# Shifting the weight tiles by 16 and 48 bytes, and the streamed tiles to multiples of 64 bytes

## The chip, the cores and the metric

The kernel runs on one core of one Trainium2 chip. The metric is the device time in microseconds (us) of one execution, the median of several runs; smaller is better. The profiled execution shown here is one further execution of the same program, with a time stamp for each instruction.

## What is computed

One decoder block for a sequence of 512 tokens with width 1024, in float32, depth 1. Cut to what matters:

```python
h = rms_norm(x, g_mix)
u, q, k, v, gate = split(h @ w_in)                 # 1024 x 3072
y = concat(causal_pool(u), diff_attention(rope(q), rope(k), v))
x = x + (y * sigmoid(gate)) @ w_out
x = x + cross_attention(rms_norm(x, g_cross), rms_norm(mem, g_mem), w_cq, w_ckv) @ w_co
x = x + square(relu(rms_norm(x, g_mlp) @ w_up)) @ w_down   # 1024 x 4096 x 1024
out = rms_norm(x, g_final)
```

## The kernel before, in words

Almost all of the time goes into matrix products. To keep float32 precision on TensorE, each operand is split into two parts, `hi` (the value rounded to the matmul's float32r type) and `lo` (the rest), and each product is made of three matmuls: hi x hi, hi x lo, lo x hi. That is `mm3`, lines 94, 95 and 96. A matmul consists of two instructions: a weight load (LDWEIGHTS) puts a 128 x 128 stationary block into the array, and the MATMUL then streams the moving operand, here 512 columns per partition (256 in some stages). The weight load for the next matmul runs while the present one streams.

Weights come in blocks of 128 x 1024 (512 KB). `load` (line 134) brings a block into a `wraw` buffer by a DMA of SyncE's queue; `prep` (line 144) splits it: ScalarE writes `whi` (line 100), VectorE writes `wlo` (line 101). There are three buffers each of `wraw`, `whi` and `wlo`. `weights` keeps the loads three blocks ahead and the splits two blocks ahead of use. `tile_mm` (line 240) runs one block: eight k-slices of 128 columns, three matmuls each, 24 matmuls in all, weights stationary, activations moving.

The stages in order: the V projection (`v_proj`, 4 blocks: here the activations `xg` are stationary and the weight parts are moving, 96 matmuls); 20 blocks of the table `PLAN` (q, k, gate and pooling projections, moving `xg`, 480 matmuls) with the attention work threaded in between; the output projection (moving `mix`, 192); memory keys (stationary weights, moving `s`, 256 columns wide, 192); memory values (`mem_v`, stationary `s`, moving weight parts, 96); cross attention's query projection (moving `xg`, 192), its scores (`mix` moving, `s` stationary, 256 wide, 96) and its products with the values (`at` moving, `mix` stationary, 48); its output projection (moving `xg`, 192); and the MLP in four groups, each of eight up blocks (moving the normed operand, which lies in `mix`, 192 matmuls) and eight down blocks (moving the activations, which lie in `xg`, 192; the last block of all is done in two halves of 256 columns).

The instruction order on TensorE is written by hand (the code's order); the other engines follow through semaphores.

**Where the tiles lie.** All SBUF tiles come from one pool. They are laid one behind the other in the order in which a tag is first asked for, each buffer rounded up to a multiple of 32 bytes per partition. A tile of 4 bytes (`eps`, `[P, 1]`) therefore takes 32 bytes and moves all that follows by half of 64, until the next such tile (`gsub`, `[P, 1]`) moves it back. In the program before, the start addresses modulo 64 are:

| tile | role in matmuls | start mod 64 |
|---|---|---|
| `tmp`, `cst` | moving in small products, transposes | 0 |
| `onef`, `ones`, `ss`, `wraw` | `ones` stationary in the norm sums | 32 |
| `xg` | moving (q, k, gates, pooling, cq, co, down); stationary in `v_proj` | 32 |
| `whi`, `wlo` | stationary; moving in `v_proj` and `mem_v` | 32 |
| `rstd`, `vr` | `vr` stationary in attention | 32 |
| `s`, `at`, `mix` | moving and stationary; `mix` moving in out and up | 0 |

Slices of a tile begin at multiples of 512 bytes, so they keep the tile's value. "Base" below means this start address modulo 64.

Of the kernel before, what the change touches and what calls it, by code (L numbers as in the profile page):

```python
# [12 lines left out]
F32R = mybir.dt.float32r  # L13
# [4 lines left out]
P = 128  # L18
T = 512
D = 1024  # L20
# [7 lines left out]
EPS = 1e-6  # L28
# [18 lines left out]
def block_kernel(ctx: ExitStack, tc: tile.TileContext, x0g, xT, memT, wv, wm, wckv, wpool, vecs, csts, outT):  # L47
# [14 lines left out]
    def nm(s):  # L62
        uid[0] += 1
        return f"{s}_{uid[0]}"

    def sb(tag, shape, bufs, dt=F32):
        return pool.tile(shape, dt, tag=tag, name=nm(tag), bufs=bufs)

    def tmp(dt=F32):
        return sb("tmp", [P, T], 10, dt)  # L70
# [13 lines left out]
    def f(ap):  # L84
        return ap.bitcast(F32)

    V = nc.vector
# [11 lines left out]
    def split(hi, lo, src, eng=V):  # L99
        S.copy(hi, src)  # L100
        eng.tensor_tensor(lo, src, f(hi), op=ALU.subtract)  # L101
# [11 lines left out]
    warm = ps("acc", 2)  # L113
    for j in range(WARM):
        nc.tensor.matmul(warm, idle[:, :P], idle, start=j == 0, stop=j == WARM - 1)
    eps = sb("eps", [P, 1], 1)
    V.memset(eps, EPS)
    one_f = sb("onef", [P, P], 1)
    V.memset(one_f, 1.0)
    ones = sb("ones", [P, P], 1, F32R)  # L120
    V.tensor_copy(ones, one_f)

# [1 line left out]
    blocks = []  # L124

    def add(src):
# [5 lines left out]
    def load(i):  # L132
        if i >= len(blocks) or i in raw:
            return
        r = sb("wraw", [P, D], 3)
        if i == 0:
            nc.sync.dma_start(r[:, :T], blocks[i][:, :T])
            load_x(1)
            nc.sync.dma_start(r[:, T:], blocks[i][:, T:])
        else:  # L140
            nc.sync.dma_start(r, blocks[i])
        raw[i] = r

    def prep(i):
        if i >= len(blocks) or i in ready:
            return
        load(i)
        hi = sb("whi", [P, D], 3, F32R)
        lo = sb("wlo", [P, D], 3, F32R)
        if i == 0:  # L150
            V.tensor_copy(hi[:, :T], raw[i][:, :T])
            V.tensor_tensor(lo[:, :T], raw[i][:, :T], f(hi[:, :T]), op=ALU.subtract)
            split(hi[:, T:], lo[:, T:], raw[i][:, T:])
        else:
            split(hi, lo, raw[i], G if i in WPOOL else V)
        ready[i] = (hi, lo)
# [5 lines left out]
            prep(j)  # L162
        return ready.pop(i)

# [1 line left out]
    def rsqrt(dst, ssum, scale, v, l, by=None):  # L166
        """dst = (ssum * scale + EPS) ** -0.5, times by(y) for a first factor; v and l are scratch"""
        V.tensor_scalar(v, ssum, scale, EPS, op0=ALU.mult, op1=ALU.add)
        S.activation(l, ssum, AF.Ln, bias=eps, scale=scale)
        S.activation(dst, l, AF.Exp, scale=-0.5)  # L170
        S.activation(l, dst, AF.Square)
        V.scalar_tensor_tensor(l, l, -0.5, v, op0=ALU.mult, op1=ALU.mult)
        if by is not None:
            by(dst)
        V.scalar_tensor_tensor(dst, l, 1.5, dst, op0=ALU.add, op1=ALU.mult)
# [38 lines left out]
        S.activation(hi, src, AF.Copy, scale=g)  # L214
        V.scalar_tensor_tensor(lo, src, g, f(hi), op0=ALU.mult, op1=ALU.subtract)

# [1 line left out]
    clock = [0]  # L218
    due = []

# [24 lines left out]
                first and n == 0, last and n == len(ks) - 1)  # L245
            tick()

# [1 line left out]
    WU, WQ, WK, WGATE, WOUT, WCQ, WCO = 0, 4, 8, 12, 20, 28, 36  # L249
    WUP = 44  # L250
    WDN = WUP + 32
# [25 lines left out]
    def W(*key):  # L277
        return weights(where[key])

# [1 line left out]
    xr = {0: vx[:, NG_COL:]}  # L281
    xg = {}
    ss = sb("ss", [P, T], 1)
# [18 lines left out]
            load(k // 2)  # L302
    nc.sync.dma_start(cst, csts)

# [1 line left out]
    def lambdas():  # L306
        lvec = tmp()[:, :NVEC]
        nc.gpsimd.dma_start(lvec, vecs)
        lam = sb("lam", [P, 4], 1)
        lsum = sb("lsum", [P, 4], 1)  # L310
        for j in range(2):
            b = 128 * j
            V.tensor_tensor(lvec[:, b:b + 64], lvec[:, b:b + 64], lvec[:, b + 64:b + 128], op=ALU.mult)
            V.tensor_reduce(lsum[:, j:j + 1], lvec[:, b:b + 64], axis=AX.X, op=ALU.add)
            S.activation(lam[:, j:j + 1], lsum[:, j:j + 1], AF.Exp)
        V.tensor_tensor(lam[:, 2:3], lam[:, 0:1], lam[:, 1:2], op=ALU.subtract)
        V.tensor_scalar(lam[:, 3:4], lam[:, 2:3], LAM_INIT, None, op0=ALU.add)
        gsub = sb("gsub", [P, 1], 1)
        V.tensor_scalar(gsub, vec[:, GSUB:GSUB + 1], 1.0 - LAM_INIT, None, op0=ALU.mult)
        st["lam"], st["gsub"] = lam[:, 3:4], gsub  # L320

# [1 line left out]
    def v_proj():  # L323
        o = [ps("sc", 3), ps("sc", 3), ps("sc", 3), ps("av", 1)]
        tbs = [slice(i * P, (i + 1) * P) for i in range(NT)]
        for b in range(4):
            wh, wl = W("v", b)
            for kk in range(2):
                k = 2 * b + kk
                if k not in xg:  # L330
                    x_in(k)
                c = slice(kk * T, (kk + 1) * T)
                for i, tb in enumerate(tbs):
                    nc.tensor.matmul(o[i], xg[k][0][:, tb], wh[:, c], start=k == 0, stop=False)  # L334
                for i, tb in enumerate(tbs):
                    nc.tensor.matmul(o[i], xg[k][1][:, tb], wh[:, c], start=False, stop=False)  # L336
                for i, tb in enumerate(tbs):
                    nc.tensor.matmul(o[i], xg[k][0][:, tb], wl[:, c], start=False, stop=k == KC - 1)  # L338
                accumulate(ss, k, xr[k])
        sp = split_sq(ss, T)  # L340

        def stats():
            r = rstd_full(sp, ss)
            st["rstd"] = r
            rr = rstd_rows(sp, NT)
            V.tensor_tensor(cos_r, cos_r, r, op=ALU.mult)
            V.tensor_tensor(sin_r, sin_r, r, op=ALU.mult)
            vs = []
            for i in range(NT):
                vh = sb("vr", [P, T], 8, F32R)  # L350
                vl = sb("vr", [P, T], 8, F32R)
                scaled(vh, vl, o[i], rr[:, 2 * i:2 * i + 1])
                vs.append((vh, vl))
            st["v"] = vs
            lambdas()

        after(3, stats)

# [1 line left out]
    def qk_proj(which, h):  # L360
        o = acc()
        tile_mm(o, W(which, h), xg)
# [16 lines left out]
            nc.sync.dma_start(f(z[bot, :, :]), f(s[top, :, :]))  # L379
            st["z", h] = z  # L380

# [1 line left out]
    def scores(h, i):  # L383
        q, k, z = st["q", h], st["k", h], st["z", h]
        n = P * (i + 1)
# [50 lines left out]

        after(FINISH, finish)

# [1 line left out]
    gate, mixed, pooled = {}, {}, {}  # L440

    def gate_proj(m):
# [18 lines left out]
        split(pr[:, 0, :], pr[:, 1, :], y, MLO_E if m < 4 else V)  # L461
        mixed[m] = (pr[:, 0, :], pr[:, 1, :])

# [1 line left out]
    def pool_weights():  # L465
        r = sb("wraw", [P, D], 3)[:, :T]
        nc.sync.dma_start(r, wpool)
# [44 lines left out]
                after(START + SPACE * j, scores, j // NT, j % NT)  # L512
        tiles[kind](m)

# [1 line left out]
    res = {}  # L516

    def residual(m, o, g=None, ss=None, nxt=None, tag=None):
# [23 lines left out]
            tile_mm(o, W(key, m), rhs, early + late)  # L542
            done(m, o)

# [1 line left out]
    def mem_in():  # L546
        mg = {}
        sm = sb("ssm", [P, M], 1)
# [44 lines left out]
            scaled(p[:, 0, :], p[:, 1, :], o[i], st["mrow"][:, 2 * i:2 * i + 1])  # L593
            st["mv", half, i] = (p[:, 0, :], p[:, 1, :])

# [1 line left out]
    ss1 = sb("ss", [P, T], 1)  # L597
    x1g = {}

# [15 lines left out]

    after(STAT1, stats1)

# [1 line left out]
    cross_o = {}  # L619

    def cross_scores(h):
# [81 lines left out]

    after(STAT2, stats2)

# [1 line left out]
    ss3 = sb("ss", [P, T], 1)  # L707
    y3 = {}

    def last_rows(m, o, c):  # L710
        """Columns c of the last residual tile, then the final norm of those tokens."""
        w = c.stop - c.start
        V.tensor_tensor(res[m][:, c], o[:, c], res[m][:, c], op=ALU.add)
        sq = tmp()[:, :w]
        S.activation(sq, res[m][:, c], AF.Square)
        S.activation(y3[m // 2][:, 1, c], res[m][:, c], AF.Copy, scale=vec[:, G_FINAL + m:G_FINAL + m + 1])  # L716

        def norm():
            s = ps("tr", 2)[:, :w]
            nc.tensor.matmul(s, ones, st["sp3"][0][:, c], start=True, stop=False)  # L720
            nc.tensor.matmul(s, ones, st["sp3"][1][:, c], start=False, stop=False)
            nc.tensor.matmul(s, one_f, sq, start=False, stop=True)
            r, v, l = tmp()[:, :w], tmp()[:, :w], tmp()[:, :w]
            with tc.high_priority():
                S.activation(l, s, AF.Ln, bias=eps, scale=1.0 / D)
                S.activation(r, l, AF.Exp, scale=-0.5)
                V.tensor_scalar(v, s, 1.0 / D, EPS, op0=ALU.mult, op1=ALU.add)
                V.tensor_tensor(l, r, r, op=ALU.mult)
                V.scalar_tensor_tensor(l, l, -0.5, v, op0=ALU.mult, op1=ALU.mult)
                V.scalar_tensor_tensor(r, l, 1.5, r, op0=ALU.add, op1=ALU.mult)  # L730
            for j in range(KC // 2):
                for i in range(2):
                    eng = G if 2 * j + i in ON_POOL[c.start > 0] else V
                    eng.tensor_tensor(y3[j][:, i, c], y3[j][:, i, c], r, op=ALU.mult)  # L734
                nc.sync.dma_start(outT[:, 2 * j:2 * j + 2, c], y3[j][:, :, c])

        after(4, norm)

    for g in range(NG):
# [10 lines left out]
        for m in range(KC):  # L750
            last = g == NG - 1
# [3 lines left out]
            if last and m == KC - 1:  # L755
                st["sp3"] = split_sq(ss3, T)
                for hf, o in enumerate((ps("sc", 3), ps("sc", 3))):
                    c = slice(hf * M, (hf + 1) * M)
# [7 lines left out]
            if last:  # L766
                accumulate(ss3, m, res[m])
                S.activation(y3[m // 2][:, m % 2, :], res[m], AF.Copy,
                             scale=vec[:, G_FINAL + m:G_FINAL + m + 1])
# [70 lines left out]
```

## Time and profile before

| | us |
|---|---|
| median of 3 runs | 746.96 |
| lowest, highest | 746.91, 747.18 |
| span of the profiled execution (first to last instruction) | 744.6 |

The profiled execution's own time beyond its span is not given; the median is 2.4 us above the span, which is what lies around the instructions.

How to read the profile: PE is TensorE's matmul, PEld its weight load, DVE VectorE, ACT ScalarE, POOL GpSimd, SP SyncE. `L94 PE MATMUL acc<-mix,whi 128*128 128x512 f32 x296 | 117.0, 395` is a group: line 94, output tile `acc`, inputs `mix` (moving) and `whi` (stationary), 296 instructions, 117.0 us busy, 395 ns the mean of one. Matmuls are pipelined, and a matmul's shown duration reaches into the next one's; what one matmul costs is the distance from its start to the next start. That distance is read from the timeline view, whose first two columns are the start and the duration in us.

### The profile page before, as it was taken

What the parts mean: (1) busy time and instruction counts of PE and PEld (TensorE: products, weight loads), DVE (VectorE), ACT (ScalarE), POOL (GpSimd) and SP (SyncE); (2) the same over time, 40 slices, a digit from 0 to 9 for tenths busy, and PEclk for the clock granted to TensorE, in tenths of its full rate; (3) what the DMA queues carried; (4) which work ended last, traced back from release to release, by engine and by line L of the source; (5) the groups of instructions that cost most, each with busy time, mean ns of one, the idle gap of its engine ahead of it and who ended that gap; (6) DMA issues with size and microseconds to landing.
All of it is one profiled execution on the core that took longest, in us unless ns stands there. A gap on an engine that the chain in (4) does not pass through costs nothing.

```text
span 744.6 us, 8888 instructions
## 1 busy us (share of the span) xinstructions
PE 726.1 (98%) x3384; PEld 598.4 (80%) x3384; DVE 430.2 (58%) x677; ACT 354.9 (48%) x589; POOL 58.7 (8%) x50
## 2 busy tenths in 40 slices
PE   8999999999999999999999999999999999999993
PEld 6878888788889888888888888888888888888882
DVE  7587899875978556564664433443334533345436
ACT  7498997776765435344453411333214422234332
POOL 0053113533000000000000000000000000000003
PEclk9999999999999999999999999999999999999997
DMA  8343223241535531201323223233232232222203
GB/s 320 132 124 103 85 72 113 86 165 62 189 99 188 181 136 58 85 29 42 129 85 111 87 89 110 85 92 106 85 112 86 85 112 86 97 101 86 85 0 113
DMA packets 24650, 78.41 MB, mean 105 GB/s; under 512 B 2688, under 2 KB 4736, under 8 KB 24608
## 3 DMA queue, kind: packets, MB, share of 16 engines
q1 hardware_dynamic: 24560, 77.73, 32.0%
q8 instruction: 26, 0.43, 0.3%
q14 instruction: 16, 0.13, 0.1%
q0 software_dynamic: 48, 0.13, 0.0%
HBM read 73.65 MB, written 2.10 MB: 102 GB/s over the span
## 4 chain that ended last, share of the span: by engine, by line
PE 88%; ACT 5%; DVE 4%; DMA 1%; issue 1%; POOL 0%; SPq 0%; DVEq 0%; ACTq 0%
PE acc L94 25%; PE acc L96 24%; PE acc L95 24%; PE sc L96 3%; PE sc L94 3%; PE sc L95 3%; ACT tmp L395 1%; DVE mix L734 1%; DMA tmp<-xT 1%; ACT whi L100 1%; PE sc L334 1%; PE sc L336 1%; PE sc L338 1%; ACT tmp L365 1%; DVE tmp L393 1%
## 5 line engine op out<-in xcount | busy, mean ns | idle before, releaser
L100 ACT CAST whi<-wraw 128x1024 fp32r<-128x1024 f32 (+1 forms) x128 | 133.9, 1047 | 301.6 <-PE acc L95 233.2
L94 PE MATMUL acc<-xg,whi 128*128 128x512 f32 x504 | 198.6, 394 | 0.0
L96 PE MATMUL acc<-xg,wlo 128*128 128x512 f32 x504 | 196.7, 390 | 0.0
L95 PE MATMUL acc<-xg,whi 128*128 128x512 f32 x504 | 196.2, 389 | 0.0
L101 DVE TENSOR_TENSOR wlo<-wraw,whi 128x1024 fp32r<-128x1024 f32 (+1 forms) x128 | 158.2, 1236 | 32.3 <-ACT whi L100 31.2
L94 PE MATMUL acc<-mix,whi 128*128 128x512 f32 x296 | 117.0, 395 | 0.0
L96 PE MATMUL acc<-mix,wlo 128*128 128x512 f32 x296 | 116.9, 395 | 0.0
L95 PE MATMUL acc<-mix,whi 128*128 128x512 f32 x296 | 116.9, 395 | 0.0
L96 PEld LDWEIGHTS acc<-xg,wlo 128*128 128x128 f32 x504 | 94.6, 188 | 20.2
L94 PEld LDWEIGHTS acc<-xg,whi 128*128 128x128 f32 x504 | 94.7, 188 | 19.0
L95 PEld LDWEIGHTS acc<-xg,whi 128*128 128x128 f32 x504 | 94.7, 188 | 18.7
L520 DVE TENSOR_TENSOR vr<-acc,vr 128x512 f32<-128x512 f32 x41 | 28.3, 691 | 109.6 <-PE acc L96 109.6
L745 DVE SCALAR_TENSOR_TENSOR tmp<-acc,rstd 128x512 f32<-128x512 f32 x32 | 22.2, 693 | 87.6 <-PE acc L96 87.5
L96 PEld LDWEIGHTS acc<-mix,wlo 128*128 128x128 f32 x296 | 55.5, 187 | 13.6
L94 PEld LDWEIGHTS acc<-mix,whi 128*128 128x128 f32 x296 | 55.5, 187 | 13.5
L95 PEld LDWEIGHTS acc<-mix,whi 128*128 128x128 f32 x296 | 55.5, 187 | 13.5
L734 POOL TENSOR_TENSOR mix<-mix,tmp 128x256 f32<-128x256 f32 x7 | 6.1, 903 | 552.1 <-ACT mix L716 550.9
L101 DVE TENSOR_TENSOR xg<-tmp,xg 128x512 fp32r<-128x512 f32 x32 | 22.1, 692 | 0.3 <-ACT xg L100 0.3
L395 ACT ACTIVATE tmp<-tmp,small 128x128 f32<-128x128 f32 (+3 forms) x32 | 17.9, 560 | 5.8 <-DVE small L393 5.6
L100 ACT CAST xg<-tmp 128x512 fp32r<-128x512 f32 x32 | 19.8, 621 | 0.9
L746 ACT ACTIVATE tmp<-tmp 128x512 f32<-128x512 f32 x32 | 20.2, 633 | 0.0
L211 DVE TENSOR_TENSOR ss<-ss,tmp 128x512 f32<-128x512 f32 x27 | 18.5, 686 | 1.6 <-ACT tmp L210 1.4
(229 smaller groups left out, 945.1 us busy)
## 6 DMA issues: line engine op xcount, KB each, us to landing
wraw<-wm SPq DMA_DIRECT2D x108, 512.0 KB, 3.3
wraw<-wckv SPq DMA_DIRECT2D x16, 512.0 KB, 3.9
s<-s SPq DMA_DIRECT2D x8, 256.0 KB, 3.6
vr<-xT SPq DMA_DIRECT2D x8, 256.0 KB, 4.8
outT<-mix SPq DMA_DIRECT2D x8, 256.0 KB, 2.2
tmp<-xT SPq DMA_DIRECT2D x7, 256.0 KB, 6.7
wraw<-wv SPq DMA_DIRECT2D x3, 512.0 KB, 7.0
tmp<-memT SPq DMA_DIRECT2D x4, 256.0 KB, 4.7
```

Of the source, the lines that this page charges most:

```text
L94: nc.tensor.matmul(o, lh, rh, start=start, stop=False)
L95: nc.tensor.matmul(o, lh, rl, start=False, stop=False)
L96: nc.tensor.matmul(o, ll, rh, start=False, stop=stop)
L100: S.copy(hi, src)
L101: eng.tensor_tensor(lo, src, f(hi), op=ALU.subtract)
L211: V.tensor_tensor(ss, ss, sq, op=ALU.add)
L334: nc.tensor.matmul(o[i], xg[k][0][:, tb], wh[:, c], start=k == 0, stop=False)
L395: S.activation(e[:, :n], e[:, :n], AF.Exp, bias=mn, scale=-1.0, accum_out=sm[:, c:c + 1])
L520: V.tensor_tensor(t, o, t, op=ALU.add)
L734: eng.tensor_tensor(y3[j][:, i, c], y3[j][:, i, c], r, op=ALU.mult)
L745: V.scalar_tensor_tensor(t, o, 0.0, st["r2"], op0=ALU.max, op1=ALU.mult)
L746: S.activation(t, t, AF.Square)
```

## The change

The two 4-byte tiles become 64 bytes long, so that all that follows them starts at a multiple of 64. The weight tiles become 64 bytes longer (1040 columns in place of 1024), and the block inside begins at column 4 (16 bytes) in `whi` and at column 12 (48 bytes) in `wlo`:

```diff
-    eps = sb("eps", [P, 1], 1)
+    eps = sb("eps", [P, 16], 1)[:, :1]
...
-        hi = sb("whi", [P, D], 3, F32R)
-        lo = sb("wlo", [P, D], 3, F32R)
+        hi = sb("whi", [P, D + 16], 3, F32R)[:, 4:D + 4]
+        lo = sb("wlo", [P, D + 16], 3, F32R)[:, 12:D + 12]
...
-        gsub = sb("gsub", [P, 1], 1)
+        gsub = sb("gsub", [P, 16], 1)[:, :1]
```

The rest of the diff removes comments. No instruction is added, removed or moved on any of the five engines: the order of the built program is the same row for row, with the same shapes. Only addresses differ. After the change, modulo 64:

| pair (moving, stationary) | stages | before | after |
|---|---|---|---|
| `xg`, `whi` / `wlo` | plan, cq, co, down | 32, 32 | 0, 16 / 48 |
| `mix`, `whi` / `wlo` | out, up | 0, 32 | 0, 16 / 48 |
| `whi` / `wlo`, `xg` | `v_proj` | 32, 32 | 16 / 48, 0 |
| `whi` / `wlo`, `s` | `mem_v` | 32, 0 | 16 / 48, 0 |
| `s`, `whi` / `wlo` (256 wide) | memory keys | 0, 32 | 0, 16 / 48 |
| `mix`, `s` (256 wide); `at`, `mix` | cross attention | 0, 0 | 0, 0 |
| `at`, `vr` | attention's values | 0, 32 | 0, 0 |

In a triple of `mm3` with stationary weights, two matmuls use `whi` and one `wlo`.

## The prediction

> **What bounds the kernel now.** I read the page first: the busy shares, then the chain that ended last, then the costliest groups.
>
> ```profile
> PE 726.1 (98%) x3384; PEld 598.4 (80%) x3384; DVE 430.2 (58%) x677; ACT 354.9 (48%) x589; POOL 58.7 (8%) x50
> PE 88%; ACT 5%; DVE 4%; DMA 1%; issue 1%; POOL 0%; SPq 0%; DVEq 0%; ACTq 0%
> L94 PE MATMUL acc<-xg,whi 128*128 128x512 f32 x504 | 198.6, 394 | 0.0
> L94 PE MATMUL acc<-mix,whi 128*128 128x512 f32 x296 | 117.0, 395 | 0.0
> L94 PE MATMUL sc<-mix,whi x24: 393/396/399, 171.2 to 187.3; 128*128 128x512 f32 x24
> L94 PE MATMUL sc<-xg,whi x48: 278/389/475, 262.2 to 730.8; 128*128 128x512 f32 x32, 128*128 128x256 f32 x16
> L94 PE MATMUL acc<-s,whi 128*128 128x256 f32 x64 | 18.0, 281 | 0.0
> ```
>
> TensorE is busy for 98% of the span and holds 88% of the chain, and its groups have no idle time before them (the last column is 0.0). So the time is the number of matmuls times the distance between their starts. The groups stand three times each (lines 94, 95, 96). With stationary weights and moving `xg`, 512 wide: 3 x 504 + 3 x 32 = 1608. With moving `mix`: 3 x 296 + 3 x 24 = 960. Memory keys: 3 x 64 = 192 of 256 columns. The two stages in which weight parts are moving have 96 each (counted in the code).
>
> The mean durations, 394 and 395 ns, hide what matters, since they overlap. The timeline shows the starts. First the MLP: the first down matmul of group one of four, the first up matmul of group two, and that group's first down matmul; 192 matmuls lie between each two.
>
> ```profile
> 421.51 0.40 PE L94 MATMUL acc<-xg,whi 128*128 128x512 f32 x1
> 465.07 0.40 PE L94 MATMUL acc<-mix,whi 128*128 128x512 f32 x1
> 509.87 0.40 PE L94 MATMUL acc<-xg,whi 128*128 128x512 f32 x1
> ```
>
> Down: (465.07 - 421.51) / 192 = **226.9 ns** a matmul. Up: (509.87 - 465.07) / 192 = **233.3 ns**. Same shapes, same weight tiles, same line of code. What differs is the moving tile: `xg` has base 32 like the weights, `mix` has base 0. To tell the bases from the stage I look at other pairs: 12 matmuls of `v_proj` (bases 32 and 32), 24 of `mem_v` (moving 32, stationary 0), 6 of cross attention's products (0 and 0), and two 256-wide stretches, 42 matmuls of the memory keys (0 and 32) and 15 of the cross scores (0 and 0).
>
> ```profile
> 20.67 0.84 PE L336 MATMUL sc<-whi,xg 128*128 128x512 f32 x3
> 23.39 0.84 PE L336 MATMUL sc<-whi,xg 128*128 128x512 f32 x3
> 244.71 0.40 PE L94 MATMUL sc<-whi,s 128*128 128x512 f32 x1
> 250.31 0.40 PE L94 MATMUL sc<-whi,s 128*128 128x512 f32 x1
> 323.43 0.39 PE L94 MATMUL acc<-at,mix 128*128 128x512 f32 x1
> 324.79 0.39 PE L94 MATMUL acc<-at,mix 128*128 128x512 f32 x1
> 227.92 0.28 PE L94 MATMUL acc<-s,whi 128*128 128x256 f32 x1
> 232.82 0.28 PE L94 MATMUL acc<-s,whi 128*128 128x256 f32 x1
> 319.70 0.28 PE L94 MATMUL sc<-mix,s 128*128 128x256 f32 x1
> 321.50 0.28 PE L94 MATMUL sc<-mix,s 128*128 128x256 f32 x1
> ```
>
> These give 2.72 / 12 = 226.7, 5.60 / 24 = 233.3, 1.36 / 6 = 226.7, 4.90 / 42 = 116.7 and 1.80 / 15 = 120.0 ns. So for 512 columns it is not where a tile lies that counts but how the two bases differ: equal (32/32 or 0/0) gives 226.7, 32 apart (either way round) gives 233.3. For 256 columns it is the reverse: 120.0 equal, 116.7 apart.
>
> From equal bases: 512 columns less 256 columns is 226.7 - 120.0 = 106.7 ns, the price of 256 columns by themselves. Each matmul then loses something to the weight load beside it: 226.7 - 213.3 = 13.3 ns (equal, both widths), 20.0 ns (apart, 512 wide), 10.0 ns (apart, 256 wide). That loss, some 2760 times in 512-wide products, is what the change can touch.
>
> **The change part by part.** It adds and removes no instruction. All the edits come down to one unknown: the spacing when the bases are 16 or 48 apart, which no pair of this kernel has. Bounds: from below, no loss at all, 213.3 ns; from above the dearest settled row, 233.3 ns (nothing excludes a dearer one, but no row shows it). Both neighbours of 16 and 48 are known (0 and 64: 13.3 ns; 32: 20.0 ns), so a straight line between them says 16.7. Against the line speaks that the loss does not follow the distance: 32 apart costs more than equal at 512 columns and less at 256. [...] I take **10.0 ns**, the value of the memory keys, the one row in which unequal bases are cheaper: 213.3 + 10.0 = 223.3 ns for 512 columns, 116.7 for 256. This is a choice between ends far apart, not a measured thing.
>
> The sum at 10.0 ns, against the median of 746.96 (the span, 744.6, and 2.4 us around it, which stays):
>
> - `xg` moving outside the plan: (1608 - 480) x (226.9 - 223.3) = -4.1 us.
> - `xg` moving in the plan, 480 matmuls: 480 x 3.6 = 1.7 us, of which I take half, -0.9, by the row below.
> - `mix` moving: 960 x (233.3 - 223.3) = -9.6 us.
> - `v_proj`: 96 x 3.4 = -0.3 us. `mem_v`: 96 x 10.0 = -1.0 us.
> - Memory keys: 116.7 stays. The last block's 48 halves: 120.0 to 116.7, -0.2 us.
>
> Together -16.1 us, so 746.96 - 16.1 = **730.9**, say 731 us.
>
> ```profile
> 30.00:170.00 140.00, 136.56 (x649) 112.44 (x648) 117.90 (x253) 117.73 (x235) 46.06 (x34) 1.00 0.33 104
> 464.00:508.00 44.00, 44.00 (x190) 35.37 (x189) 20.02 (x23) 16.57 (x22) 0.00 (x0) 1.00 0.29 91
> 728.00:744.60 16.60, 4.21 (x30) 3.56 (x29) 10.91 (x20) 3.42 (x8) 6.14 (x7) 0.71 0.38 126
> L100 ACT CAST whi<-wraw 128x1024 fp32r<-128x1024 f32 x127 | 133.3, 1050 | 301.5 <-PE acc L95 233.2 <-issue 37.6 <-PE sc L95 15.0
> L101 DVE TENSOR_TENSOR wlo<-wraw,whi 128x1024 fp32r<-128x1024 f32 x127 | 157.5, 1241 | 32.3 <-ACT whi L100 31.2
> ```
>
> The columns of the first three rows (the windows view) are the stretch and its length, then busy time of PE, PEld, DVE, ACT and POOL, the granted clock, the DMA share and GB/s. In the plan, DVE and ACT are busy for 118 of 140 us (84%): there a faster TensorE finds its next operands not always ready, hence the half. In an MLP stretch they have 20.0 and 16.6 of 44 us, and DMA a share of 0.29: with a block of 24 matmuls at 223.3 ns (5.36 us) the split of the next one (1.05 us on ACT, 1.24 on DVE) is still covered more than four times over, and ACT's casts wait for TensorE (233.2 us), not the other way round. The tail behind 728 us is DVE, POOL and output DMA, and stays.
>
> The shifted addresses also meet ACT, DVE and the DMAs. For those I take nothing, by these rows, a write to base 32 and one to base 0:
>
> ```profile
> L214 ACT ACTIVATE xg<-vr,vx 128x512 fp32r<-128x512 f32 x8 | 5.8, 720 | 0.4 <-DVE vr L520 0.4
> L214 ACT ACTIVATE mix<-vr,vx 128x512 fp32r<-128x512 f32 x8 | 5.7, 718 | 0.3 <-DVE vr L520 0.3
> L215 DVE SCALAR_TENSOR_TENSOR xg<-vr,vx,xg 128x512 fp32r<-128x512 f32 x8 | 6.0, 745 | 0.0
> L215 DVE SCALAR_TENSOR_TENSOR mix<-vr,vx,mix 128x512 fp32r<-128x512 f32 x8 | 6.0, 745 | 0.0
> ```
>
> 720 against 718 ns and 745 against 745: no difference. Were the covered casts 10% dearer (0.1 us each), the cover above takes it, except in the plan, where 20 blocks would cost up to 20 x 0.23 = 4.6 us; nothing in the rows points there.
>
> **The rivals.**
>
> *Slower: unequal is unequal.* Bases 16 and 48 apart lose 20.0 ns like 32 apart, in every 512-wide stage. Then `mix` and `mem_v` gain nothing and `xg` goes from 226.9 to 233.3: 1608 x 6.4 = +10.3 us (none of it hidden, the plan's too, as TensorE holds the chain), `v_proj` 96 x 6.6 = +0.6, the halves -0.2: 746.96 + 10.7 = 757.7. For it: the only unequal distance in the trace behaves so, in three stages. Against it: the 256-wide rows. It decides from 229.4 ns on: that is where 1704 matmuls at 226.9 (`xg`, `v_proj`) lose what 1056 at 233.3 (`mix`, `mem_v`) gain.
>
> *Midway.* The straight line, 230.0 ns: `xg` 1608 x 3.1 = +5.0, `mix` 960 x 3.3 = -3.2, `v_proj` and `mem_v` cancel, keys 192 x 1.6 = +0.3: +2.1, 749.1 us.
>
> *Only the half of 64 bytes counts.* Then 16 is as good as equal, and 48 as bad as 32: a triple has two at 226.7 and one at 233.3, mean 228.9. `xg` 1608 x 2.0 = +3.2, `mix` 960 x 4.4 = -4.2, `v_proj` +0.2, `mem_v` -0.4, keys 192 x 2.2 = +0.4: -0.8, 746.2 us. The rows can't exclude it, as all bases in them are 0 or 32.
>
> *As good as equal.* 16 and 48 both give 226.7: `mix` 960 x 6.6 = -6.3, `mem_v` -0.6, keys 192 x 3.3 = +0.6: -6.3, 740.6 us. That is also what equal bases everywhere would give.
>
> *Much better.* Half of the smallest loss equal bases show is left, 6.7 ns: 220.0 ns. A further 3.3 ns on all: 731 - 9 = 722 us. With no loss left it would be about 703.
>
> *The change does nothing.* The spacings of up and down would then have to come from the stage, not from the bases; `v_proj`, `mem_v` and cross attention speak against it. 747 us. The Trainium skill, "TensorE: Matmul & The Clock Gate", section "Step-by-step: what each phase is for", has a rule on this side: it says that TensorE has two independent read ports and that loading the next weights takes no read bandwidth from the running matmul. By that rule no base can matter and the time stays at 747; the trace disagrees, with 226.9 and 233.3 ns in two neighbouring MLP stretches.
>
> **How the numbers follow.** Chances: 10 ns loss (731) 0.34; much better (722) 0.10; as good as equal (740.6) 0.16; half of 64 bytes (746.2) 0.12; midway (749.1) 0.08; unequal is unequal (757.7) 0.17; nothing (747) 0.03. A measurement of this kernel can tell about 0.2%, 1.5 us, from no change. Faster by more: 0.34 + 0.10 + 0.16, and 0.05 of the half-of-64 case, 0.65. Within: 0.07 of that case, 0.03 of nothing and 0.02 of midway, 0.12. Slower: 0.06 of midway and 0.17, 0.23. The range has to take in 757.7, whose 0.17 with the tail below 718 would leave out about 2 in 10: 718 to 758, so that about 1 in 10 is outside. The faster cases by themselves lie between 718 and 742.
>
> **What would show it.** In the changed kernel's timeline: the distance from the first down matmul of an MLP group to the first up matmul of the next (43.56 us now) and from there to the next down matmul (44.80 us). Both at 42.9 us is my case. Both equal whatever their size shows that only the difference of the bases counts, as `xg` and `mix` then have the same one; a difference of 1.2 us that remains shows that the stage was the cause. Both at 44.8 is the slower rival, 43.5 the "as good as equal" one, 43.9 the half-of-64 one. Inside a triple, lines 94, 95 and 96 show whether 16 and 48 differ. The prediction is wrong if the loss per load does not fall, or if the plan takes longer because ACT's or DVE's casts into the shifted tiles do.

## The result and the profile after

| | before | after |
|---|---|---|
| median, us (lowest to highest of 4 runs) | 747.07 (746.91 to 747.37) | 751.72 (751.00 to 752.64) |
| span of the profiled execution, us | 744.6 | 750.9 |

The ratio is 1.0063, with a 95% interval of 1.0049 to 1.0076: the change makes the kernel **0.63% slower**. Forecast was 731 us. The time lies inside the range of 718 to 758, but on the other side of the time before. (One of e2's executions further down ran at a mean granted clock of 0.654 and took 1040.58 us; it is left out of e2's range, and e2's spacings come from another profile of the same kernel.)

The page of the changed kernel, the same lines as before: busy shares, the chain, the two largest groups of matmuls, and the two splits of the weights (group: busy us, mean ns, then idle time before).

```profile
PE 731.3 (97%) x3384; PEld 599.3 (80%) x3384; DVE 430.2 (57%) x677; ACT 354.3 (47%) x589; POOL 58.8 (8%) x50
PE 89%; DVE 5%; ACT 2%; DMA 1%; issue 1%; POOL 0%; SPq 0%; DVEq 0%
L94 PE MATMUL acc<-xg,whi 128*128 128x512 f32 x504 | 200.6, 398 | 0.0
L94 PE MATMUL acc<-mix,whi 128*128 128x512 f32 x296 | 117.0, 395 | 0.0
L100 ACT CAST whi<-wraw 128x1024 fp32r<-128x1024 f32 x127 | 132.9, 1047 | 306.6 <-PE acc L95 235.9 <-issue 41.1 <-PE sc L95 15.3
L101 DVE TENSOR_TENSOR wlo<-wraw,whi 128x1024 fp32r<-128x1024 f32 x127 | 157.6, 1242 | 31.9 <-ACT whi L100 30.8
```

TensorE still holds the chain (89%), and its busy time has grown by 5.2 us (731.3 against 726.1). The splits into the shifted tiles take what they took (1047 and 1242 ns; 1050 and 1241 before). So the time went where it was looked for, into the spacing of the matmuls. The timeline of the changed kernel (start, duration) at the first down, up, down, up and down matmul of successive MLP stretches, 192 matmuls apart:

```profile
425.26 0.40 PE L94 MATMUL acc<-xg,whi 128*128 128x512 f32 x1
469.74 0.40 PE L94 MATMUL acc<-mix,whi 128*128 128x512 f32 x1
514.28 0.40 PE L94 MATMUL acc<-xg,whi 128*128 128x512 f32 x1
558.58 0.39 PE L94 MATMUL acc<-mix,whi 128*128 128x512 f32 x1
603.27 0.40 PE L94 MATMUL acc<-xg,whi 128*128 128x512 f32 x1
```

Down: 44.48 / 192 = 231.7 ns, and in the next group 44.30 / 192 = 230.7 (226.9 before). Up: 44.54 / 192 = 232.0 ns and 44.69 / 192 = 232.8 (233.3 before). `mix` gained about 1 ns a matmul here, `xg` lost 4 to 5. Added up from start to start over the whole trace, the products with moving `xg` took 5.9 us more, `v_proj` 1.6 us more, those with moving `mix` 1.1 us less, `mem_v` 0.3 us less and the memory keys 0.3 us more: 6.4 us, where the span grew by 6.2.

Of the 1.6 us in `v_proj`, 1.1 are not spacing but one longer wait, before its 25th matmul (first line before, second after; in brackets the idle time):

```profile
11.46 0.50 PE L334 MATMUL sc<-whi,xg 128*128 128x512 f32 x1 [0.75 <-ACT whi L100]
13.01 0.50 PE L334 MATMUL sc<-whi,xg 128*128 128x512 f32 x1 [1.88 <-ACT whi L100]
```

After the change ScalarE, which writes that `whi`, had itself waited 1.76 us for a DMA of the input `x`. In the six profiled kernels e1 to e6 below, the time from the start of the 24th to that of the 25th matmul is 0.56 to 1.39 us (1.14 before, 2.27 after), whatever their addresses. The longer wait also helps to explain why the span of the profiled execution grew by 6.2 us and the median by 4.7: that execution is the longest of the four (752.64 us).

### The profile page after: what moved, and what is told of

Its sections match the earlier page's. It is cut to its first block, busy times and chain, and to the rows that moved or that the text cites. A ratio compares the mean times of both kernels' runs of the same rounds, so it can differ in the third digit from the quotient of the medians.

```text
span 750.9 us, 8888 instructions
## 1 busy us (share of the span) xinstructions
PE 731.3 (97%) x3384; PEld 599.3 (80%) x3384; DVE 430.2 (57%) x677; ACT 354.3 (47%) x589; POOL 58.8 (8%) x50
## 4 chain that ended last, share of the span: by engine, by line
PE 89%; DVE 5%; ACT 2%; DMA 1%; issue 1%; POOL 0%; SPq 0%; DVEq 0%
PE acc L94 25%; PE acc L95 25%; PE acc L96 25%; PE sc L94 3%; PE sc L96 3%; PE sc L95 3%; DMA tmp<-xT 1%; DVE mix L734 1%; PE sc L334 1%; DVE tmp L393 1%; PE sc L336 1%; PE sc L338 1%; ACT tmp L365 1%; PE av L95 0%; ACT whi L100 0%
## 5 line engine op out<-in xcount | busy, mean ns | idle before, releaser
L94 PE MATMUL acc<-xg,whi 128*128 128x512 f32 x504 | 200.6, 398 | 0.0
L95 PE MATMUL acc<-xg,whi 128*128 128x512 f32 x504 | 198.3, 394 | 0.0
L520 DVE TENSOR_TENSOR vr<-acc,vr 128x512 f32<-128x512 f32 x41 | 28.4, 692 | 113.7 <-PE acc L96 113.6
```

The costliest lines, as they stand in the source:

```text
L94: nc.tensor.matmul(o, lh, rh, start=start, stop=False)
L95: nc.tensor.matmul(o, lh, rl, start=False, stop=False)
L520: V.tensor_tensor(t, o, t, op=ALU.add)
```

## The experiments

Three theories were set against each other at first: (A) the difference of the starts modulo 64 decides, as the prediction has it; (B) a longer period decides; (C) some distance gives less than 226.7 ns. "Distance" is from here on the start of the stationary block minus the start of the moving one, **modulo 256**, which the first experiment turns out to give. Read from the built programs:

| stage | before | after (the three buffers of each part) |
|---|---|---|
| moving `xg` | 0 | `whi` 16, 80, 144; `wlo` 240, 48, 112 |
| moving `mix` | 224 | `whi` 80, 144, 208; `wlo` 48, 112, 176 |
| `mem_v` | 32 | 176, 112, 48; 208, 144, 80 |

In the column "after" the three buffers differ because a tile of 1040 columns is 4160 bytes long, 64 more than a multiple of 256.

**m1: a map of the distances.** The kernel computes nothing of the block: it runs 48 matmuls at each distance, with the same operand shapes.

```diff
+    for d in list(range(0, 512, 16)) + [0, 4, 8, 12, 20, 24, 28, 36, 48, 60]:
+        block(m % KC, d, 48)
...
+            nc.tensor.matmul(o[:, :w], whi[:, c + k * P:c + (k + 1) * P], xg[:, k, i % 2, :w],
```

> Measures the disputed cost by itself and computes nothing of the block: 42 stretches of 48 matmuls of 512 columns, then 16 stretches of 48 of 256 columns, back to back with no other work, each stretch with one fixed distance (stationary start less moving start) of 0 to 496 bytes in steps of 16, then of 0 to 60 in steps that are no multiples of 16. Theory A (only the distance modulo 64 counts): the settled spacing repeats every 64 bytes, 226.7 ns at 0, 64, 128 and so on, about 232 at 16 and 48, 233.3 at 32. Theory B (the old equal pairs were quick because they were equal in a much longer period, all 32768 apart): 226.7 at 0 and near it alone, some 232 nearly everywhere else, 64 and 128 included. Theory C (my prediction's choice): somewhere at 16 or 48 a spacing near 223.

Timeline of the map, each row 38 (512 wide) or 37 (256 wide) matmuls in a row; the second column is the time from the first start to the last end. The rows are, from the top, distances of 0, 16, 48, 64, 128, 192, 240 and 256 bytes, then 0 and 64 bytes at 256 columns.

```profile
18.32 8.79 PE L91 MATMUL acc<-xg,whi 128*128 128x512 f32 x38
29.21 8.78 PE L91 MATMUL acc<-xg,whi 128*128 128x512 f32 x38
51.35 9.03 PE L91 MATMUL acc<-xg,whi 128*128 128x512 f32 x38
62.54 9.03 PE L91 MATMUL acc<-xg,whi 128*128 128x512 f32 x38
107.30 9.03 PE L91 MATMUL acc<-xg,whi 128*128 128x512 f32 x38
151.89 8.86 PE L91 MATMUL acc<-xg,whi 128*128 128x512 f32 x38
185.28 8.78 PE L91 MATMUL acc<-xg,whi 128*128 128x512 f32 x38
196.16 8.78 PE L91 MATMUL acc<-xg,whi 128*128 128x512 f32 x38
484.31 4.60 PE L91 MATMUL acc<-xg,whi 128*128 128x256 f32 x37
507.01 4.36 PE L91 MATMUL acc<-xg,whi 128*128 128x256 f32 x37
```

Less the last one's own 0.39 or 0.40 us (0.28 at 256 columns), and by 37 or 36 spacings: 8.78 gives 226.8 ns, 8.86 gives 228.9, 9.03 gives 233.2; at 256 columns 120.0 and 113.3. The single starts in the trace give the settled values a little finer (each distance was entered in one way here, from the stretch before it; m3 below shows that this can matter):

| distance | 0 | 16 | 32 | 48 | 64 | 80 | 96 | 112 to 160 | 176 | 192 | 208, 224 | 240 | 256 |
|---|---|---|---|---|---|---|---|---|---|---|---|---|---|
| ns, 512 wide | 226.7 | 226.7 | 233.3 | 233.3 | 233.3 | 231.9 | 234.3 | 233.3 | 230.0 | 228.9 | 233.3 | 226.7 | 226.7 |

From 256 to 496 the same values come again. Distances that are no multiple of 16 are not quick either: 232.4 ns at 4 bytes, 230.7 at 8, 230.0 at 12, 231.1 at 24, 235.0 at 28, the highest of the map. So (A) falls: 64 and 128 bytes apart are not "equal" but cost 233.3 ns. (B) holds, with a period of 256 bytes, and (C) falls: nothing at 512 columns is below 226.7. The rows of before fit: 0 in `xg`, `v_proj` and cross attention's products (226.7), 224 in `mix` and 32 in `mem_v` (233.3). Every "equal" pair of before was in fact a multiple of 256 apart. And it is the difference that counts, not where the weights start: equal pairs are at 226.7 ns with both starts 224 modulo 256 (`xg` before) and with both 0 (here).

**e1: the alignment alone.** The two small tiles get 64 bytes, the weight tiles stay as they were.

```diff
-    eps = sb("eps", [P, 1], 1)
+    eps = sb("eps", [P, 16], 1)[:, :1]
...
-        gsub = sb("gsub", [P, 1], 1)
+        gsub = sb("gsub", [P, 16], 1)[:, :1]
```

> Only the two 4-byte tiles lengthened to 64 bytes; weight tiles as before, no shift inside them. All bases are 0 modulo 64. The weights stay at a multiple of 4096 from xg, and come to 448 modulo 512 from mix. Theory A: 226.7 ns everywhere, 740 to 741 us. Theory B: xg stays at 226.9 ns, mix goes from 233.3 to about 232, 745 to 747 us.

742.91 us, ratio 0.9943 (0.9928 to 0.9957). Distances: `xg` 0, `mix` 192. First down, up and down of its timeline:

```profile
419.48 0.39 PE L94 MATMUL acc<-xg,whi 128*128 128x512 f32 x1
463.02 0.40 PE L94 MATMUL acc<-mix,whi 128*128 128x512 f32 x1
506.99 0.40 PE L94 MATMUL acc<-xg,whi 128*128 128x512 f32 x1
```

Down 43.54 / 192 = 226.8 ns, up 43.97 / 192 = 229.0, the map's value for 192. This half of the change is a gain: 960 matmuls x (233.3 - 229.0) = 4.1 us, and 4.2 were measured. The time lies between the two forecasts, 740 to 741 (A) and 745 to 747 (B), and meets neither, as `mix` came to 229.0 ns and not to 226.7 or 232. The other half of the change must cost the remaining 8.8 us (751.72 - 742.91).

**e2: the longer tile alone.** As the changed kernel, but both parts begin at column 0.

```diff
-        hi = sb("whi", [P, D + 16], 3, F32R)[:, 4:D + 4]
-        lo = sb("wlo", [P, D + 16], 3, F32R)[:, 12:D + 12]
+        hi = sb("whi", [P, D + 16], 3, F32R)[:, :D]
+        lo = sb("wlo", [P, D + 16], 3, F32R)[:, :D]
```

> The changed kernel without the 16 and 48 bytes: the weight tiles keep their 64 extra bytes, but the block begins at byte 0 of each. All bases are 0 modulo 64, but the distances modulo 512 are 0 to 320 in steps of 64, another for each buffer. Theory A: 226.7 ns everywhere, 740 to 741 us, so the shift is to blame. Theory B: the length is to blame, about 232 ns as in the changed kernel, 750 to 753 us.

751.06 to 751.64 us in four runs, ratio 1.0057 (1.0040 to 1.0073). The spacings are read from a further run of the same kernel, which took 751.19 us:

> The same kernel as e2_pitch once more, for a profile at the full clock. By m1_map: distances of whi 0, 64, 128 and of wlo 192, 0, 64 from xg, 64 more from mix, one set for each of the three buffers, so in most blocks 229 to 233 ns, 231 to 232 on average for both, as in the changed kernel; 751 us.

```profile
423.88 0.39 PE L94 MATMUL acc<-xg,whi 128*128 128x512 f32 x1
468.17 0.39 PE L94 MATMUL acc<-mix,whi 128*128 128x512 f32 x1
512.73 0.40 PE L94 MATMUL acc<-xg,whi 128*128 128x512 f32 x1
```

Down 230.7 ns, up 232.1: nearly the changed kernel's values, without any shift. The 64 extra bytes per buffer are enough: the three buffers then lie at distances 0, 64 and 128 (`whi`) and 192, 0 and 64 (`wlo`) from `xg`, and only some of the loads are at a quick one.

**m2: triples of unlike loads.** As m1, but the three matmuls of a triple have distances of their own, 96 in a row. It computes nothing of the block.

```diff
+    for ds in ((0, 0, 0), (16, 16, 16), (16, 16, 48), (0, 0, 48), (0, 0, 64), (0, 0, 128), (16, 16, 240),
+               (80, 80, 48), (144, 144, 112), (208, 208, 240), (208, 208, 176), (192, 192, 192)):
+        block(m % KC, ds, 96)
```

> Computes nothing of the block: 12 stretches of 96 matmuls of 512 columns in triples like mm3 (distances of the first, second and third load from the moving tile, modulo 256), then four stretches of 16 weight blocks of 24 matmuls whose distances go round the three buffers as in the changed kernel for xg and for mix, and as in e2_pitch for xg and for mix. If the distance of each load alone decides, a mixed triple has the mean of the single distances of m1_map: (0,0,48) 228.9 ns, (16,16,48) 228.9, (16,16,240) 226.7, (80,80,48) 232.4, (144,144,112) 233.3, (192,192,192) 228.9; the changed kernel's rounds 230.8 for xg and, with 208 and 176 in them, 231.9 for mix. If one unlike load of three breaks the settled state, (0,0,48) and (16,16,48) are at 231 or more, and the rounds nearer 232.

Its timeline for (0, 0, 0), (16, 16, 48), (0, 0, 48) and (16, 16, 240), 62 matmuls each:

```profile
20.98 14.22 PE L91 MATMUL acc<-xg,whi 128*128 128x512 f32 x62
64.62 14.63 PE L91 MATMUL acc<-xg,whi 128*128 128x512 f32 x62
87.00 14.56 PE L91 MATMUL acc<-xg,whi 128*128 128x512 f32 x62
153.75 14.77 PE L91 MATMUL acc<-xg,whi 128*128 128x512 f32 x62
```

226.7, 233.3, 232.3 and 235.6 ns. One unlike load in three takes away the gain of all three: (0, 0, 48) would be 228.9 as a mean of single values (two at 226.7, one at 233.3), and is 232.3. And (16, 16, 240), all three quick in the map, is the slowest of all. The spacings of a mixed sequence are no mean of those of its parts. Three more values of this run: (192, 192, 192) settled at 233.3 ns, not at the map's 228.9; the round of three buffers as in the changed kernel ran at 233.4 ns for `xg` (230.8 was forecast, and the kernel's down stretches have 230.7 to 231.7) and at 231.9 for `mix` (231.9 forecast, 231.9 to 232.8 in the kernel). So the distances alone don't give the spacing of a mixed round either.

**e3: the shift alone.** As e1, with the blocks of each part in one tile of 3 x 1024 + 64 columns, so that they lie 4096 bytes apart, and begin at 16 and 48 bytes.

```diff
+    whi = sb("whi", [P, 3 * D + 64], 1, F32R)
+    wlo = sb("wlo", [P, 3 * D + 64], 1, F32R)
...
+        c = (i % 3) * D
+        hi, lo = whi[:, c + 4:c + D + 4], wlo[:, c + 12:c + D + 12]
```

Because the blocks share a tile here, in the output projection and cross attention's output projection late k-slices of the first three blocks are multiplied with weights of later blocks; the instructions and their sizes stay. That holds for e5 and e6 too.

> e1_align with the shift alone: 16 bytes in whi, 48 in wlo, but the blocks stay 4096 bytes apart (three blocks lie in one tile for each part). Distances modulo 256: xg 16, 16, 48; mix 208, 208, 240. If each load's distance alone decides: xg 228.9 ns (1608 x 2.2 = 3.5 us more than e1_align), mix 231.1 (960 x 2.2 = 2.1), memory keys 0.9, 749 to 750 us. If the 48 breaks the settled state for the whole triple: 233 for xg, 754 to 758 us. If a shift costs nothing as long as the blocks lie 4096 apart: 743 us as e1_align.

752.92 us, ratio 1.0074 (1.0054 to 1.0094).

```profile
424.31 0.40 PE L94 MATMUL acc<-xg,whi 128*128 128x512 f32 x1
469.09 0.39 PE L94 MATMUL acc<-mix,whi 128*128 128x512 f32 x1
513.47 0.40 PE L94 MATMUL acc<-xg,whi 128*128 128x512 f32 x1
```

Down 44.78 / 192 = 233.2 ns, as (16, 16, 48) in m2; up 44.38 / 192 = 231.1, as (208, 208, 240) there (231.1). That is the spacing of the second forecast, but the time is 1 us under its range: in the plan a matmul with moving `xg` lost only 3.0 ns against e1 (480 took 113.7 us, 112.3 in e1), elsewhere 6.1. So the shift alone costs 10.0 us against e1, the length alone 8.5, and both together, the changed kernel, 8.8. They don't add up: each by itself already breaks the equal distances.

**e4: all starts equal modulo 256.** As e1, with 128 more bytes ahead of `s` and 64 ahead of `at`, so that `xg`, `mix`, `at` and all the weight parts are multiples of 256 apart.

```diff
-        gsub = sb("gsub", [P, 16], 1)[:, :1]
+        gsub = sb("gsub", [P, 48], 1)[:, :1]
...
+            if h == 0:
+                sb("gap", [P, 16], 1)
```

> e1_align with 128 more bytes ahead of s and 64 ahead of at, so that xg, mix, at, whi and wlo are equal modulo 256 and s stands 192 from them; the weight tiles as before the change, no shift. If the distance modulo 256 decides: mix goes from e1_align's 229 ns to 226.7 (960 x 2.2 = 2.1 us), mem_v from 233.3 to 228.9 (0.4), the cross scores from 120.0 to 113.3 (0.6): 739.5 to 740 us. If only the distance modulo 64 counts, nothing changes against e1_align: 742.9.

**739.12 us**, ratio 0.9889 (0.9872 to 0.9905): faster than both kernels, by a change of addresses alone.

```profile
417.67 0.39 PE L94 MATMUL acc<-xg,whi 128*128 128x512 f32 x1
461.19 0.39 PE L94 MATMUL acc<-mix,whi 128*128 128x512 f32 x1
504.70 0.39 PE L94 MATMUL acc<-xg,whi 128*128 128x512 f32 x1
```

43.52 and 43.51 / 192: both 226.6 to 226.7 ns, in every group. `mem_v`, at distance 192, has 228.9. Against the kernel before, the stages with moving `mix` took 6.3 us less, and `mem_v`, the memory keys and `xg` 0.4 us less each; the span fell by 7.8.

**e5 and e6: one shift for both parts, and none, in the shared tile.** As e3, with `wlo` at 16 bytes like `whi` (e5), and with both at 0 (e6).

```diff
-        hi, lo = whi[:, c + 4:c + D + 4], wlo[:, c + 12:c + D + 12]
+        hi, lo = whi[:, c + 4:c + D + 4], wlo[:, c + 4:c + D + 4]
```

> As the kernel with the shift alone, with one edit: the lo part begins at 16 bytes like the hi part, in place of 48. xg and all three loads of a triple are then 16 bytes apart modulo 256, mix and all three loads 208 apart. Theory 'unlike loads' (a settled quick state needs every load of a triple at a quick distance; 16 is as quick as 0, by the map): the stages with moving xg go from 233.2 to 226.7 ns, those with moving mix from 231.1 to 233.3, the sum 752.9 - 1608 x 6.5 ns + 960 x 2.2 ns = 744.5 us. Rival 'a shift off the multiples of 64 costs by itself': xg stays at 231 to 233 ns, the time at 752 us or above.

> As the kernel with the shift alone, but both parts begin at column 0 of their blocks: only the shared tile of the three blocks is left. It shows what that form costs by itself. If nothing: 742.9 us, as the kernel with the alignment alone, xg at 226.8 and mix at 228.9 ns. If the shared tile is what made the shift experiment slow: 752 us, whatever the spacings.

e6: 743.53 us, ratio 0.9950 (0.9932 to 0.9967), spacings as in e1; so the shared tile costs nothing that can be told. e5: 750.25 us, ratio 1.0039 (1.0024 to 1.0054), a miss by 5.8 us, and its timeline says why. First down, up, down, up:

```profile
424.71 0.39 PE L94 MATMUL acc<-xg,whi 128*128 128x512 f32 x1
469.51 0.40 PE L94 MATMUL acc<-mix,whi 128*128 128x512 f32 x1
514.03 0.39 PE L94 MATMUL acc<-xg,whi 128*128 128x512 f32 x1
557.55 0.39 PE L94 MATMUL acc<-mix,whi 128*128 128x512 f32 x1
```

The first down stretch takes 44.80 us, 233.3 ns a matmul, the next one 43.52, 226.7 ns: the same instructions on the same addresses, all three loads 16 bytes apart from `xg`. Cross attention's query and output projections sit at 233.3 as well, the other two down stretches at 226.7. So at 16 bytes there are two settled states, and neither theory that went in had that. The forecast had also put `mix` at 233.3 ns (it was 231.9), and had started from e3's time with the plan's 480 matmuls at full weight.

**m3: the way in.** 36 matmuls at one distance, after 5 to 8 at a slow one; 16 ways in for each of four distances. It computes nothing of the block.

```diff
+    for d in (0, 16, 240, 192):
+        for first in (128, 208, 48, 80):
+            for n in (5, 6, 7, 8):
+                block(m % KC, [first] * n + [d] * 36)
```

> Computes nothing of the block. 64 runs of matmuls: 36 at one distance (0, 16, 240 or 192 modulo 256, 16 runs each), each entered after 5, 6, 7 or 8 matmuls at a slow distance (128, 208, 48 or 80). Theory 'the way in decides': at 16 (and 240, 192) some of the 16 runs settle at 226.7 ns (192: 228.9) and others at 233.3, while all 16 runs at distance 0 settle at 226.7. Rival 'the distance alone decides': all 16 runs of a distance settle at one value, 16 at 226.7, and the 233.3 ns stages of the kernel with both parts at 16 bytes have another cause. If runs at distance 0 also settle at 233.3, equal starts are no guarantee either.

Its timeline, 26 matmuls each: distance 0; distance 16 entered after 5 and after 6 matmuls at 128; the same for 192.

```profile
58.91 6.05 PE L92 MATMUL acc<-xg,whi 128*128 128x512 f32 x26
175.25 6.06 PE L92 MATMUL acc<-xg,whi 128*128 128x512 f32 x26
184.86 6.23 PE L92 MATMUL acc<-xg,whi 128*128 128x512 f32 x26
488.25 6.23 PE L92 MATMUL acc<-xg,whi 128*128 128x512 f32 x26
498.00 6.11 PE L92 MATMUL acc<-xg,whi 128*128 128x512 f32 x26
```

(6.06 - 0.39) / 25 = 226.8 ns and (6.23 - 0.40) / 25 = 233.2, with one matmul more or less ahead. Over the 16 ways in: distance 0 settled at 226.7 every time; 16 at 226.7 four times and at 233.3 twelve times; 240 at 226.7 eight times and at about 228.3 eight times; 192 at 228.9 fifteen times and at 233.3 once. Of the four distances tried, only equal starts are quick from every way in.

## Why the prediction was wrong

**What held.** TensorE's matmuls set the time, and the number of matmuls times the spacing is the right sum: with the measured spacings it gives the measured changes (e1 4.1 for 4.2 us). ACT's and DVE's splits cost nothing extra, as taken. The half taken for the plan was near: a matmul with moving `xg` lost 2.5 ns there (480 took 112.3 us before, 113.5 after) and 4.1 outside it, though that it was the operands' readiness that hid the rest is not shown.

**The step that failed** is "I take 10.0 ns" for the loss beside the load, and the premise under it, "it is not where a tile lies that counts but how the two bases differ" modulo 64. Measured in the changed kernel, over the bare 213.3 ns, the loss is 17.4 to 18.4 ns in the down stretches and 18.7 to 19.5 in the up ones, not 10.0: the sum of -16.1 us came out as +4.7. The 10.0 was carried over from the 256-wide rows. The map shows that this was not to be had: 256 columns have another pattern (113.3 ns at 64 apart, where 512 columns have 233.3), and at 512 columns no distance measured loses less than 13.3. The 213.3 is itself an estimate that no run shows: it takes the loss at equal starts to be the same at both widths. By the map 512 columns cost 106.7 ns more than 256 at a distance of 0, but 115.6 at 192 and 120.0 at 64, so the loss is not the same at both widths in general.

**The premise** was never tested by the rows of before. Every equal pair in them was equal modulo 256 as well, and no row had 64 apart. The argument in the text ("both neighbours of 16 and 48 are known (0 and 64: 13.3 ns; 32: 20.0 ns)") took the row at 0 for one at 64. With that gone, the edit to the tile's length, 64 bytes more, was a change of its own, which the prediction's steps don't have at all; e2 shows that it alone costs 8.5 us against e1.

**The test that it named** would have misled: "both equal whatever their size shows that only the difference of the bases counts". After the change the first pair was 44.48 and 44.54 us, nearly equal (the second 44.30 and 44.69), and the conclusion would have been false. Both stretches mixed several distances, and the mixed distances measured here mostly end between 230 and 236 ns.

**The rivals.** The 749.1 us of *midway* (230.0 ns for both) is the nearest to 751.72, and the measured 230.7 to 232.8 ns lie behind the break-even of 229.4 that the slower rival named; but its ground, a straight line between neighbours, is no better than the chosen one: the map jumps from 226.7 at 16 to 233.3 at 32. *Only the half of 64 bytes counts* had the single values right by chance (16 like 0, 48 like 32) and failed on the mean, since one unlike load in three costs all three their place. *As good as equal* gave 740.6 us as the value of equal starts everywhere, and e4 measured 739.12.

**The rule of the Trainium skill** that was weighed there ("TensorE: Matmul & The Clock Gate", section "Step-by-step: what each phase is for": loading the next weights takes no read bandwidth from the running matmul) fares no better here if it is read, as there, to mean that no base can matter. With nothing but the distance changed, m1 goes from 226.7 to 235.0 ns. Whether it is read bandwidth that is lost, no run shows.

## What to carry to other kernels

Where float32r matmuls of 512 columns with a fresh weight load each run back to back, look up the built start addresses of the moving and the stationary tiles, and make them equal modulo 256 bytes, for every buffer of a rotation (a tile's length counts as much as its start). It was worth 1.1% here, and no instruction changed. At 256 columns another distance was best, 64 or 192. And where a trace shows that a quantity repeats, look for the row that would tell one period from a longer one before building on it; if no row can, an untested period belongs among the rivals.

## What the runs showed that was not expected

- The spacing of 512-wide matmuls depends on the distance with a period of 256 bytes: 226.7 ns at 0, 233.3 at 64 and 128, 228.9 at 192. At 256 columns it is quickest at 64 and 192 (113.3 ns), and equal starts are among the slowest (120.0).
- At 16 bytes two settled states exist, 226.7 and 233.3 ns, on the same addresses and in the same kernel (e5). One matmul more ahead decided between them in m3.
- What in the way in decides, and which part of the chip makes the period, no run here shows. That a load and a stream keep a fixed order in time once settled fits the two states, but is only argued. Nor is it shown why the round of the changed kernel's distances runs at 233.4 ns in m2 and at 230.7 to 231.7 in the kernel.
